# A hybrid decoder layer on one core: the first pass's places filled earlier in the queue, rotary tables and forget chain issued later, background sums spread over two stages, one place filled sooner

## The chip, the cores and the metric

The kernel runs on one core of one Trainium2 chip. The metric is the device time of one execution in microseconds. Before the change the median of three runs is 917.3 us (917.18 to 917.92).

## What is computed

A decoder layer on 512 tokens of width 2048, with two groups of eight heads side by side: FoX heads (attention with a forget term added to the logits) and MLA heads (latent attention with a rotary part). Cut to what matters:

```python
def _hybrid_layer(x, cos, sin, g_pre, w_in, g_q, w_uq, g_kv, w_ukv, b_forget, w_out, g_post):
    h = _rms_norm(x, g_pre)
    proj = h @ w_in                       # 2048 x 6472
    (q_lat, kv_lat, k_rope_raw, gate_mla,
     fq, fk, fv, f_logit, gate_fox) = jnp.split(proj, split_points, axis=-1)
    o_mla = _mla_branch(q_lat, kv_lat, k_rope_raw, g_q, w_uq, g_kv, w_ukv, cos, sin) * jax.nn.silu(gate_mla)
    o_fox = _fox_branch(fq, fk, fv, f_logit, b_forget) * jax.nn.silu(gate_fox)
    o = jnp.concatenate([o_mla, o_fox], axis=-1) @ w_out
    return x + _rms_norm(o, g_post)
# _fox_branch: log_f = log_sigmoid(f_logit + b_forget); c = cumsum(log_f);
#   logits = (q . k) * scale + c[query] - c[key], causal softmax, times v
# cos, sin: of positions * inv_freq, used in the MLA heads alone
```

## The kernel before

All of it is one straight program. TensorE runs the matmuls in fp32 split into a high and a low part, so a product is three matmuls: `mm3`, L149 (high by high), L150 and L151 (high by low, low by high). Each weight block of 128x1024 numbers ("chunk", 512 KB) goes the same way: a DMA from HBM into a tile `raw`, issued on SP's queue (`load`, L249 and L262); ScalarE (ACT) rounds it to the high part `whi` (L282, about 1.05 us); VectorE (DVE) subtracts to get the low part `wlo` (L283, about 1.2 us); then TensorE (PE) uses both. Division into parts runs two chunks ahead of the matmuls. `raw` tiles come from small pools, so a load waits until what used its place before is done. Each engine works its instructions in the order of its queue; SP, which only issues DMAs, does too. SP's DMAs share eight completion semaphores in turn, so in the built program a DMA on SP also waits for the landing of the DMA eight places before it.

Large products are done in a seven-product scheme over 2x2 blocks: products p1, p2, g5, g3, g7, q6, p4 of two operands each, where operands can be sums or differences of blocks. Sums of weight blocks are made by DMA in two ways:

- **Chains** (`add_chain`, `fill`, L232): a place in memory holds a first block, loaded by SP (L235), and later products add further blocks to the same place by an accumulating DMA on GpSimd's (POOL's) queue (L237). The first pass has eight such places per pair of outputs: v0 to v3, g0 to g3; the second pair l and m has its own.
- **Background sums** (`add_step`, L310 to L327) for blocks of w_out and w_ukv, in DRAM: 16 steps, each a small mark (SP, L327), a copy of the first block (SP, L325) and an accumulate of the second (POOL, L321). Four are narrow (named ...u), twelve move 1 MB twice (...o). `paced` lets one step go after so many weight tiles (`set_pace`; a wide one takes twice as many).

Sums of x blocks are made on DVE and stored away by POOL (L993, `awaymg`), to be fetched later (L1032).

The stages, in order of time in the trace: the opening projection (`proj_first`, tiles `in`, L645, 16 steps of k, each 12 matmuls of 128x328 and 4 transposes; the normalised x comes as `h` from ACT and then from DVE, L142), fq of head pair 0, then p1 and p2 for v and g (tiles `va`, `ga`), the other five products of v and g (`products`), fk, the FoX heads in four pairs, p1 and p2 of l and m, their other products (g5 of m is tile `mg`), the latent stage, the MLA heads in four pairs, and the output projection.

Around the change:

- `rotary_tables` (L857): SP loads the inverse frequencies (L859) and four pieces of the positions (L863); DVE then casts the positions (L870), multiplies (L871) and reduces the angle in many small steps (L877 to L905), ACT takes sines, POOL stores the tables, SP spreads them (L913). Its DMAs are written where it is called, its steps where `todo` reaches them. The scheduler that orders the program outside the sections written in fixed order may place them earlier.
- `forget_sums` (L786): the forget chain, 17 small steps on DVE and ACT with a RECIPROCAL on DVE (L829) and a store of the cumulative sums to DRAM (`c_dram`, L818), read by FoX (`load_keys`). `fs[0]` runs early, `fs[1:]` where they are put into `todo`.
- `fill` for l and m: the four places of g5's l are `slot` tiles filled after p1 of l and m (L1510); the first place of g5's m, `rawm0`, is a tile of the pool `rw`, which opens only when p2 of l is done (L1524).

Of the kernel before, what the change touches and what calls it, by code (L numbers as in the profile page):

```python
# [65 lines left out]
def tile_hybrid_layer(  # L66
# [32 lines left out]
    def slot(name, dt=F32, shape=(P, 2, S)):  # L99

        return sp.tile(list(shape), dt, tag="s", name=name)
# [127 lines left out]
    def fill(i, raw):  # L229

        raws[i] = raw
        to = raw.rearrange("p (k c) -> p k c", k=2)  # L232
        first, second = chunks[i][0]
        if first is not None:
            nc.sync.dma_start(to, first)  # L235
        if second is not None:
            pool.dma_start(to, second, accum_op=ALU.add)  # L237
# [351 lines left out]
    def set_pace(n):  # L589
        state.update(pace=n, tiles=0)  # L590
# [196 lines left out]
    def forget_sums(r):  # L787
# [5 lines left out]
        def rows():  # L793
            pool.memset(zrow, 0.0)
            pt = att_bank("rf")
            for t in range(NT):
                pe.transpose(pt[:n, t * P : (t + 1) * P], r[:, t * n : (t + 1) * n], ident)
            dve.tensor_copy(rf[:n, :], pt[:n, :])
# [16 lines left out]

        def scan():
            dve.tensor_tensor_scan(rf[R, :], z, zrow, 0.0, op0=ALU.add, op1=ALU.add)
            nc.sync.dma_start(c_dram, rf[R, :])  # L818
# [437 lines left out]
    set_pace(1000)  # L1256
    rot = rotary_tables()
    todo.append(fs[0])
# [97 lines left out]
    drain()  # L1356
    todo.extend(fs[1:])
    for g in "vg":
# [6 lines left out]
        {  # L1365
            ("g5", "v"): (1, d3), ("g5", "g"): (1, f7), ("g5", "g", "after"): lambda: todo.extend(rot),
            ("g3", "v"): (1, d7), ("g3", "g"): (1, f6), ("g7", "v"): (1, d6),
# [9 lines left out]
    pp = heads_room.enter_context(tc.tile_pool(name="pp", bufs=2, reuse_waits="tile"))  # L1377
    set_pace(3.7)
    wait(4)
# [128 lines left out]
    drain()  # L1508
    for j in range(4):
        fill(prods["g5", "l"][j], slot(f"rawl{j}", shape=(P, 1024)))  # L1510
    l4 = slot("l4b", shape=(P, NT, L4))
# [10 lines left out]
    for f in f5:  # L1522
        f()
    fill(prods["g5", "m"][0], beside[0].tile([P, 1024], F32, tag="raw", name="rawm0", bufs=1))  # L1524
    raws_of[0] = slot("lat4")
# [45 lines left out]

    set_pace(4.5)
    pp = heads_room.enter_context(tc.tile_pool(name="pp", bufs=2, reuse_waits="tile"))
# [65 lines left out]
    for p in range(4):  # L1639
# [5 lines left out]
        if p == 0:  # L1645
            set_pace(4.5)
            A = [proj_bank("uA0"), bank("pv", "uA1", 1)]
# [264 lines left out]
```

## Time and profile before

| what | value |
|---|---|
| median of three runs | 917.3 us |
| the profiled execution | 922.15 us, of which its span from first to last instruction is 920.4 us |
| PE busy | 885.9 us, 96% of the span |
| DVE, ACT, POOL busy | 634.6, 499.4, 125.4 us |
| mean granted TensorE clock | 0.981 of full speed |
| DMA queues | q1 (issued by SP): 136.28 MB; q0 (issued by POOL): 61.02 MB |

How to read it: a time in a row is microseconds from the start of the span. A row of the timeline is start, duration, engine, line, operation, output and inputs, and in brackets the idle time before it with what ended it. A row of the chain of waits is start, duration and what lies on the path that ended last; a DMA there lasts from issue to landing. A row of the stretch table gives, for a stretch of time, its length, then the busy time (and instruction count) of PE, of PE's weight loads (PEld), DVE, ACT and POOL, then the granted clock (PEclk, 1.00 is full speed), the share of time that the DMA engines were busy, and GB/s. A PE busy share of 96% does not say that PE runs at full speed for 96%: in a stretch with PEclk 0.50 it is busy with the same matmuls for twice as long.

### The profile page before, as it was taken

The numbers are of one execution on the slowest core, as the hardware profiler recorded it, in microseconds if no ns is written. First come the engines' busy times: TensorE is split into PE (matmuls) and PEld (weight loads), VectorE is DVE, ScalarE is ACT, GpSimd is POOL, SyncE is SP. The second block draws the span as 40 slices with busy tenths as digits, with TensorE's granted clock in tenths as the row PEclk, the third lists the DMA queues.
The fourth block names the chain that finished last, engine by engine and source line by source line (L and its number), as shares of the span: only waits on it lengthen the run. The fifth ranks groups of instructions, "written<-read, shape, count | busy, mean of one in ns | idle before, by whom it ended". The sixth has DMA issues, their size and how long they took to land.

```text
span 920.4 us, 13773 instructions
## 1 busy us (share of the span) xinstructions
PE 885.9 (96%) x5078; PEld 779.2 (85%) x5078; DVE 634.6 (69%) x1056; ACT 499.4 (54%) x914; POOL 125.4 (14%) x133
## 2 busy tenths in 40 slices
PE   5999989999999999899997999999999999999996
PEld 5988889999988888688997999997888888887885
DVE  2789586658455553545664766899796895888786
ACT  4764554435345362444743444566866877645473
POOL 0114102442200010100022344100000000000021
PEclk8899989999999999899999999999999999999998
DMA  8979968999799999997699999652322335788878
GB/s 266 244 214 261 254 195 197 220 227 220 179 223 292 263 257 245 254 259 219 183 301 325 308 224 206 107 164 60 104 58 73 122 100 197 233 314 304 278 223 249
DMA packets 128360, 198.41 MB, mean 216 GB/s; under 512 B 16210, under 2 KB 61164, under 8 KB 127268
## 3 DMA queue, kind: packets, MB, share of 16 engines
q1 hardware_dynamic: 101300, 136.28, 46.7%
q0 software_dynamic: 26256, 61.02, 33.5%
q8 instruction: 40, 0.66, 0.3%
q10 hardware_dynamic: 736, 0.22, 0.1%
q14 instruction: 28, 0.23, 0.1%
HBM read 182.60 MB, written 44.25 MB: 246 GB/s over the span
## 4 chain that ended last, share of the span: by engine, by line
PE 79%; DMA 10%; DVE 4%; issue 3%; ACT 2%; POOL 1%; SPq 1%; DVEq 0%; ACTq 0%; POOLq 0%
DMA raw<-in_w_in_dram 4%; DMA rawm<-in_w_in_dram 3%; PE sm L688 3%; PE fq L149 3%; PE in L645 3%; PE fq L150 3%; PE fq L151 3%; PE fk L151 2%; PE fk L149 2%; PE fk L150 2%; PE mq L149 2%; PE mq L150 2%; PE mq L151 2%; PE sf L688 2%; PE oa L151 2%
## 5 line engine op out<-in xcount | busy, mean ns | idle before, releaser
L283 DVE TENSOR_TENSOR wlo<-raw,whi 128x1024 fp32r<-128x1024 f32 (+3 forms) x159 | 186.8, 1177 | 116.7 <-ACT whi L282 116.0
L282 ACT CAST whi<-raw 128x1024 fp32r<-128x1024 f32 (+3 forms) x159 | 160.6, 1012 | 153.7 <-PE fk L150 33.7
L149 PE MATMUL fk<-h,whi 128*128 128x512 f32 x128 | 52.5, 410 | 0.0
L149 PE MATMUL fq<-h,whi 128*128 128x512 f32 x128 | 52.0, 406 | 0.0
L150 PE MATMUL fq<-h,whi 128*128 128x512 f32 x128 | 50.8, 397 | 0.0
L151 PE MATMUL fq<-h,wlo 128*128 128x512 f32 x128 | 50.7, 396 | 0.0
L151 PE MATMUL fk<-h,wlo 128*128 128x512 f32 x128 | 50.3, 393 | 0.0
L150 PE MATMUL fk<-h,whi 128*128 128x512 f32 x128 | 50.0, 391 | 0.0
L1732 POOL DMA_DIRECT2D c<-in_x_dram x8 | 7.0, 1008 | 309.0 <-ACT c L1731 309.0
L282 ACT CAST whi<-rawv 128x1024 fp32r<-128x1024 f32 x24 | 25.1, 1050 | 41.5 <-PE gc L150 9.8
L282 ACT CAST whi<-rawg 128x1024 fp32r<-128x1024 f32 x24 | 25.2, 1051 | 29.7 <-PE vc L151 8.9
L283 DVE TENSOR_TENSOR wlo<-rawv,whi 128x1024 fp32r<-128x1024 f32 x24 | 29.3, 1224 | 17.1 <-ACT whi L282 17.0
L645 PE MATMUL in<-whi,h 128*128 128x328 f32 x128 | 31.0, 329 | 8.9 <-DVE h L142 8.7
L283 DVE TENSOR_TENSOR wlo<-rawg,whi 128x1024 fp32r<-128x1024 f32 x24 | 29.3, 1223 | 14.2 <-ACT whi L282 14.2
L706 ACT ACTIVATE pf<-pf,stf 128x128 f32<-128x128 f32 (+3 forms) x32 | 18.0, 562 | 33.1 <-DVE stf L697 33.1
L282 ACT CAST whi<-rawl 128x1024 fp32r<-128x1024 f32 x20 | 21.0, 1049 | 22.2 <-PE mc L150 7.5
L283 DVE TENSOR_TENSOR wlo<-rawl,whi 128x1024 fp32r<-128x1024 f32 x20 | 24.4, 1223 | 10.2 <-ACT whi L282 10.2
L645 PEld LDWEIGHTS in<-whi,h 128*128 128x128 f32 x128 | 22.0, 193 | 9.4 <-DVE h L142 9.0
L151 PEld LDWEIGHTS fq<-h,wlo 128*128 128x128 f32 x128 | 24.6, 192 | 5.6
L149 PE MATMUL mq<-ln,whi 128*128 128x512 f32 x72 | 29.0, 403 | 0.0
L151 PEld LDWEIGHTS fk<-h,wlo 128*128 128x128 f32 x128 | 24.0, 188 | 5.3
L150 PEld LDWEIGHTS fq<-h,whi 128*128 128x128 f32 x128 | 24.7, 193 | 4.5
(635 smaller groups left out, 2963.3 us busy)
## 6 DMA issues: line engine op xcount, KB each, us to landing
raw<-in_w_in_dram SPq DMA_DIRECT2D x62, 512.0 KB, 8.9
raw<-in_w_out_dram SPq DMA_DIRECT2D x32, 512.0 KB, 4.9
rawv<-in_w_in_dram POOLq DMA_DIRECT2D x16, 512.0 KB, 6.5
rawg<-in_w_in_dram POOLq DMA_DIRECT2D x16, 512.0 KB, 9.6
rawl<-in_w_in_dram POOLq DMA_DIRECT2D x16, 512.0 KB, 9.9
raw<-in_w_in_dram POOLq DMA_DIRECT2D x12, 512.0 KB, 9.7
bmg<-awaymg SPq DMA_DIRECT2D x20, 256.0 KB, 9.4
rawv<-in_w_in_dram SPq DMA_DIRECT2D x8, 512.0 KB, 4.7
```

Of the source, the lines that this page charges most:

```text
L149: pe.matmul(o, ah, bh, start=first, stop=False, **kw)
L150: pe.matmul(o, ah, bl, start=False, stop=False, **kw)
L151: pe.matmul(o, al, bh, start=False, stop=last, **kw)
L282: act.copy(hi[:, :m], raw[:, :m])
L283: dve.tensor_tensor(out=lo[:, :m], in0=raw[:, :m], in1=hi[:, :m].bitcast(F32), op=ALU.subtract)
L645: pe.matmul(banks[t][:, :n], a[k][:, tss[t]], b[:, j, :], start=k == 0 and m == 0, stop=k == NK - 1 and m == 2,)
L688: pe.matmul(s[:, :nn], a[:, qs], c[:, :nn], start=(i == 0), stop=(i == len(pairs) - 1))
L706: act.activation(p, p, AF.Exp, bias=st[:, 0:1], scale=unit, accum_out=st[:, 1:2])
L1732: pool.dma_start(to, x[piece(t, c)], accum_op=ALU.add)
```

## The change

Six edits. The SP half of `fill` is pinned to the order in which the program is written, so the scheduler may not move it behind other DMAs. The memset of `zrow` goes from the first step of the forget chain to its last. `rotary_tables` is called, and the rest of the forget chain is queued, after product g3 of g instead of at the opening and after p1. The pace of the background sums goes from 3.7 to 6 tiles in the FoX stage and from 4.5 to 3.3 in the MLA stage (a second `set_pace(4.5)` inside the MLA loop goes away). The first place of g5's m becomes a slot and is filled together with the four of l.

```diff
@@ fill
-            nc.sync.dma_start(to, first)
+            in_order(nc.sync.dma_start(to, first))
@@ forget_sums
         def rows():
-            pool.memset(zrow, 0.0)
...
         def scan():
+            pool.memset(zrow, 0.0)
@@
     set_pace(1000)
-    rot = rotary_tables()
     todo.append(fs[0])
@@
     drain()
-    todo.extend(fs[1:])
     for g in "vg":
         one("p2", g, A[g], False, side=f3 if g == "g" else ())
@@ products("vg", {
-            ("g5", "v"): (1, d3), ("g5", "g"): (1, f7), ("g5", "g", "after"): lambda: todo.extend(rot),
+            ("g5", "v"): (1, d3), ("g5", "g"): (1, f7), ("g3", "g", "after"): lambda: todo.extend([*fs[1:], *rotary_tables()]),
@@ FoX stage
-    set_pace(3.7)
+    set_pace(6)
@@ after p1 of l and m
-    for j in range(4):
-        fill(prods["g5", "l"][j], slot(f"rawl{j}", shape=(P, 1024)))
+    for i in (*prods["g5", "l"], prods["g5", "m"][0]):
+        fill(i, slot(f"rawl{i}", shape=(P, 1024)))
@@
     for f in f5:
         f()
-    fill(prods["g5", "m"][0], beside[0].tile([P, 1024], F32, tag="raw", name="rawm0", bufs=1))
@@ MLA stage
-    set_pace(4.5)
+    set_pace(3.3)
@@
         if p == 0:
-            set_pace(4.5)
```

What this does to the order of the built program shows at three places. First SP's queue in the opening, before: `bcol` is the forget bias, `ifc` the inverse frequencies, `angles` the positions, `rawv` and `rawg` are first-pass places, `raw_152` and `raw_157` are chunks 5 and 6 of the opening projection (k = 8, 9 and k = 10, 11).

```order
L766 DMA bcol<-in_b_forget_dram 8x1
L859 DMA ifc<-in_inv_freq_dram 128x2
L863 DMA angles<-in_positions_dram 32x128 x4
L235 DMA rawv_678<-in_w_in_dram 128x2x512
L235 DMA rawv_680<-in_w_in_dram 128x2x512
L262 DMA raw_152<-in_w_in_dram 128x2x320
L262 DMA raw_152<-in_w_in_dram 128x2x8
L235 DMA rawv_682<-in_w_in_dram 128x2x512
L235 DMA rawv_684<-in_w_in_dram 128x2x512
L262 DMA raw_157<-in_w_in_dram 128x2x320
L262 DMA raw_157<-in_w_in_dram 128x2x8
L235 DMA rawg_686<-in_w_in_dram 128x2x512
```

And the same stretch of SP's queue after the change.

```order
L766 DMA bcol<-in_b_forget_dram 8x1
L235 DMA rawv_670<-in_w_in_dram 128x2x512
L235 DMA rawv_672<-in_w_in_dram 128x2x512
L235 DMA rawv_674<-in_w_in_dram 128x2x512
L235 DMA rawv_676<-in_w_in_dram 128x2x512
L262 DMA raw_152<-in_w_in_dram 128x2x320
L262 DMA raw_152<-in_w_in_dram 128x2x8
L235 DMA rawg_678<-in_w_in_dram 128x2x512
L859 DMA ifc<-in_inv_freq_dram 128x2
L262 DMA raw_157<-in_w_in_dram 128x2x320
L262 DMA raw_157<-in_w_in_dram 128x2x8
L863 DMA angles<-in_positions_dram 32x128 x4
```

The positions are still loaded in the opening, though `rotary_tables` is called much later in the text: the scheduler hoists them. They have moved from ahead of all five places to behind them and behind chunks 5 and 6.

Second, DVE's queue at the same place, before: `h3` to `h7` are the normalised x of steps k = 3 to 7, `wlo3` the low part of chunk 3 (k = 4, 5).

```order
L283 TENSOR_TENSOR wlo2_237<-raw2_135,whi2_236 128x656
L870 CAST angles_672<-angles_672 128x128
L871 TENSOR_SCALAR angles_672<-angles_672,ifc_670 128x128
L877 TENSOR_SCALAR angles_672<-angles_672 128x128
L878 TENSOR_SCALAR angles_672<-angles_672 128x128
L142 SCALAR_TENSOR_TENSOR h3_261<-xt3_256,gcol_124,h3_261 128x512
L885 SCALAR_TENSOR_TENSOR angles_672<-angles_672 128x128 x4
L877 TENSOR_SCALAR angles_672<-angles_672 128x128
L878 TENSOR_SCALAR angles_672<-angles_672 128x128
L142 SCALAR_TENSOR_TENSOR h4_285<-xt4_280,gcol_124,h4_285 128x512
L283 TENSOR_TENSOR wlo3_289<-raw3_142,whi3_288 128x656
```

And after: `h8` and `wlo5` belong to step k = 8.

```order
L283 TENSOR_TENSOR wlo3_289<-raw3_142,whi3_288 128x656
L142 SCALAR_TENSOR_TENSOR h5_313<-xt5_308,gcol_124,h5_313 128x512
L142 SCALAR_TENSOR_TENSOR h6_321<-xt6_316,gcol_124,h6_321 128x512
L283 TENSOR_TENSOR wlo4_346<-raw4_147,whi4_345 128x656
L142 SCALAR_TENSOR_TENSOR h7_354<-xt7_349,gcol_124,h7_354 128x512
L870 CAST angles_1719<-angles_1719 128x128
L871 TENSOR_SCALAR angles_1719<-angles_1719,ifc_1717 128x128
L142 SCALAR_TENSOR_TENSOR h8_378<-xt8_373,gcol_124,h8_378 128x512
L877 TENSOR_SCALAR angles_1719<-angles_1719 128x128
L878 TENSOR_SCALAR angles_1719<-angles_1719 128x128
L885 SCALAR_TENSOR_TENSOR angles_1719<-angles_1719 128x128 x3
L283 TENSOR_TENSOR wlo5_403<-raw5_152,whi5_402 128x656
```

The cast of the positions, which waits for their four DMAs, has moved on DVE's queue from ahead of `h3` to behind `h7` and ahead of `h8` and `wlo5`.

Third, POOL's queue between the FoX stage and the product `mg`, before: `t6o` and `t4o` are background sums, `rawl` the places of l, `rawm` the first place of m, `raw_4420`, `raw_4469` and `raw_4520` its second to fourth, `awayoa` and `awayog` stores.

```order
L321 DMA t6o_115<-t7o_111 128x2048
L321 DMA t4o_119<-t6o_115 128x2048
L993 DMA awayoa_4761<-gc_1106 256x1x256
L237 DMA rawl_4335<-in_w_in_dram 128x2x512
L237 DMA rawl_4338<-in_w_in_dram 128x2x512
L237 DMA rawl_4341<-in_w_in_dram 128x2x512
L237 DMA rawl_4344<-in_w_in_dram 128x2x512
L237 DMA raw_4420<-in_w_in_dram 128x2x512
L993 DMA awayoa_4907<-gc_1105 256x1x256
L993 DMA awayog_4832<-rog_4817 128x1024
L993 DMA awayog_4868<-rog_4853 128x1024
L237 DMA rawm_4578<-in_w_in_dram 128x2x512
```

And after, where `rawl_4329` is the first place of m and `raw_4405`, `raw_4454` and `raw_4505` its second to fourth.

```order
L321 DMA t7o_110<-in_w_out_dram 128x2x1024
L993 DMA awayoa_4743<-gc_1097 256x1x256
L237 DMA rawl_4317<-in_w_in_dram 128x2x512
L237 DMA rawl_4320<-in_w_in_dram 128x2x512
L237 DMA rawl_4323<-in_w_in_dram 128x2x512
L237 DMA rawl_4326<-in_w_in_dram 128x2x512
L237 DMA rawl_4329<-in_w_in_dram 128x2x512
L993 DMA awayoa_4889<-gc_1096 256x1x256
L237 DMA raw_4405<-in_w_in_dram 128x2x512
L993 DMA awayog_4814<-rog_4799 128x1024
L993 DMA awayog_4850<-rog_4835 128x1024
L237 DMA raw_4454<-in_w_in_dram 128x2x512
```

The accumulate of m's first place has moved up on POOL, past that of its second place, a store of 256 KB and two stores of 512 KB. Its third still stands behind all of those stores.

## The prediction, on record before the run

> **What bounds the kernel now.** First the page.
>
> ```profile
> span 920.4 us, 13773 instructions
> PE 885.9 (96%) x5078; PEld 779.2 (85%) x5078; DVE 634.6 (69%) x1056; ACT 499.4 (54%) x914; POOL 125.4 (14%) x133
> ```
>
> TensorE (PE) is the bound, so an edit can pay only where PE waits or runs at a lower clock. The view of waits, for PE alone, says where: engine, line and awaited work, then microseconds in total, times, longest.
>
> ```profile
> PE in L645 <- DVE h L142: 8.7, 1, 8.7
> PE mg L149 <- ACT whi L282: 5.3, 1, 5.3
> PE ga L151 <- DVE wlo L283: 2.4, 1, 2.4
> PE pvf L149 <- ACT phf L138: 2.3, 1, 2.3
> ```
>
> Four single stalls stand out, 18.7 us together. The table of stretches shows that they cost more than that.
>
> ```profile
> 17.86:28.10 10.24, 4.04 (x17) 4.00 (x17) 5.35 (x16) 0.59 (x1) 0.00 (x0) 0.50 0.87 275
> 116.84:123.67 6.83, 5.68 (x26) 5.68 (x27) 5.84 (x7) 1.93 (x3) 0.88 (x2) 0.50 0.61 194
> ...
> 111.40:128.84 17.44, 14.62 (x96) 14.04 (x95) 15.04 (x17) 7.49 (x10) 1.44 (x2) 0.80 0.62 204
> 315.58:320.52 4.94, 4.94 (x27) 4.16 (x25) 4.94 (x11) 2.49 (x5) 0.00 (x0) 1.00 1.05 248
> 369.05:381.09 12.04, 8.80 (x27) 6.65 (x26) 7.69 (x19) 4.46 (x10) 1.57 (x2) 0.72 0.97 281
> 487.20:498.62 11.42, 11.42 (x98) 11.42 (x96) 5.02 (x6) 3.93 (x6) 3.63 (x3) 1.00 1.07 342
> 498.62:518.40 19.78, 14.04 (x99) 13.55 (x98) 12.87 (x16) 8.26 (x10) 2.46 (x4) 0.83 1.08 326
> ...
> 667.00:745.00 78.00, 77.37 (x392) 64.37 (x391) 65.24 (x135) 57.62 (x141) 0.00 (x0) 1.00 0.27 82
> 262.00:369.00 107.00, 107.00 (x511) 88.80 (x510) 56.27 (x126) 51.49 (x109) 9.19 (x10) 1.00 0.99 259
> ```
>
> The first two rows are half-clock stretches (PEclk 0.50): each stall is followed by one, and a stretch of 6.83 us at half clock loses 3.4 us of work. The next five are products with and without their stall. A product of 96 matmuls of this size takes 11.42 us at full speed (`lg`, 487.20). `ga` of p2 (111.40) took 17.44, so its stall and low clock cost 6.0. The FoX piece at 369.05 took 12.04 against 4.94 for the same 27 matmuls a pair earlier: 7.1. `mg` (498.62) took 19.78: 8.4.
>
> The trace and a rule differ here: the stall of 2.4 us in `ga` was enough to bring 6.83 us at clock 0.50. The Trainium skill, page "TensorE: Matmul & The Clock Gate", section "HAM oscillation — how this bites in real kernels", gives as abstract rule that idle gaps over some 3.4 us are to be avoided; this row shows a shorter one doing it. By that rule a leftover stall below 3.4 us would cost only its own length; by the row it can cost 3.4 more.
>
> **Opening: the stall moves.** Rows of the chain of waits, of the timelines of PE, DVE and SP, and of the DMA view from 15.5 to 19 us.
>
> ```profile
> 18.51 3.68 DMA angles<-in_positions_dram
> 34.98 1.77 PE in L645 x12
> 37.19 1.80 PE in L645 x12
> ...
> 14.47 0.85 PE L645 MATMUL in<-whi,h 128*128 128x328 f32 x4
> 24.06 1.46 PE L645 MATMUL in<-whi,h 128*128 128x328 f32 x4 [8.74 <-DVE h L142]
> ...
> 22.27 0.23 DVE L870 CAST angles<-angles 128x128 f32<-128x128 int32 x1 [9.80 <-DMA angles<-in_positions_dram]
> 23.26 0.74 DVE L142 SCALAR_TENSOR_TENSOR h<-xt,gcol,h 128x512 fp32r<-128x512 f32 x1
> 23.92 1.26 DVE L885 SCALAR_TENSOR_TENSOR angles<-angles 128x128 f32<-128x128 f32 x4
> 26.28 0.83 DVE L283 TENSOR_TENSOR wlo<-raw,whi 128x656 fp32r<-128x656 f32 x1
> ...
> 20.00 1.80 SPq L235 DMA_DIRECT2D rawv<-in_w_in_dram  x2
> ...
> DMA packets 1267, 1.21 MB, mean 346 GB/s; under 512 B 81, under 2 KB 1267, under 8 KB 1267
> ```
>
> DVE stood 9.80 us at the cast of the positions, whose DMAs lay behind x on SP's queue until 22.19 (18.51 + 3.68); the x of step k = 3 stood behind the cast, and PE behind that, from 15.3 to 24.06. After the change the cast stands behind `h7`, so k = 3 to 7 run without it. A step takes 2.21 us (34.98 to 37.19), so k = 8 could start at 15.3 + 5 x 2.21 = 26.4 instead of 37.19: 10.8 us, if nothing else held it. But the positions now stand on SP's queue behind five places of 512 KB and two chunks of 336 KB, 3.29 MB; at 346 GB/s that is 9.5 us. Added to the old landing, 31.7; if the whole 3.68 us of their own issue and landing overlapped with it, 28.0. I take 30. The Trainium skill, page "DMA: Bandwidth & Descriptors", section "Anatomy of one DMA", fits 2.0 us plus bytes at 436 GB/s for a DMA from the other queue; as an estimate that is 7.5 us for the 3.29 MB, and the term below would be about 4 instead of 2; this row, with 346 GB/s in small packets, is slower.
>
> From the cast DVE needs 1.73 us to the end of an `h` (22.27 to 24.00, with L871 to L878 between), 0.95 for three L885 (1.26 x 3/4) and 0.83 for `wlo5`: 3.5. So `wlo5`, which k = 8 needs for its second matmul, is there at 33.5. The half clock then goes on, as before (28.10 is 4.0 us after 24.06, which lost 2.0). So k = 8 stands where it would have started at about 35.5, against 37.19: **a gain of 1.7**, from -1 (31.7 and a longer half clock) to 5 (28.0 and a shorter one). ACT's sines and the table store come later in the opening, beside running matmuls; nothing for those.
>
> **p2 of g.** Rows of the chain, of the timelines of SP, POOL and DVE, and of the DMA view at 93.2 us.
>
> ```profile
> 98.23 11.66 DMA awaymg<-rmg
> 110.42 4.78 DMA raw<-in_w_in_dram
> ...
> 97.39 14.72 SPq L249 DMA_DIRECT2D raw<-in_w_in_dram  x5
> ...
> 93.26 0.59 POOL L993 DMA_DIRECT2D awaymg<-rmg  x1
> ...
> 113.33 3.35 DVE L829 RECIPROCAL fd<-fd 8x512 f32<-8x512 f32 x1
> ...
> awaymg<-rmg POOLq DMA_DIRECT2D x1, 512.0 KB, 11.1
> ```
>
> Of the five loads from 97.39 on, the last three left SP only after the last away store had landed (98.23 + 11.66 = 109.89), because the third one's place overlaps that store's. One of them, issued at 110.42, landed at 115.2, and DVE was then in the forget chain's RECIPROCAL until 116.68. In the changed program the places fall otherwise: the chunk for the start of `ga` waits for the store before (93.26 + 11.1 = 104.4), the next two only for DVE, and the fourth alone for 109.89. With the 4.78 us of the row it lands by 114.7, and the fourth quarter of `ga` starts at 111.40 + 3 x 2.85 = 119.95, with 1.05 us of rounding ahead. The chain of RECIPROCAL is gone from here. **Gain 5.5**, bounds 0 (the same queue delay meets the second quarter) and 6.0.
>
> The forget chain now runs in product g7. One row on the room there.
>
> ```profile
> 175.00:205.00 30.00, 30.00 (x179) 26.82 (x178) 19.07 (x21) 12.46 (x14) 13.66 (x12) 1.00 1.11 223
> ```
>
> DVE is idle for 10.9 of 30 us and division runs two chunks (5.7 us) ahead, so 3.35 us hide: 0, at worst 1. FoX reads the sums only after two more products, q6 and p4.
>
> **FoX.** One row of the chain:
>
> ```profile
> 345.44 24.86 DMA raw<-in_w_in_dram
> ```
>
> This load took 24.86 us from issue to landing while the DMA engines were busy 0.99 of the time (262 to 369). It shares them with a background step. At pace 6 instead of 3.7 there are 38% fewer of these; seven of the twelve wide steps stay in FoX. PE waited 2.3 us and a little more behind it, so 21 us would be soon enough: 16% less. **Gain 6.5** of 7.1; bounds 0 (what holds it is SP's own queue, with keys and values ahead) and 7.1.
>
> **m's first place.** Rows of the chain, of POOL's timeline and of the DMA view at 461.3 and 465.8 us.
>
> ```profile
> 476.54 10.89 DMA rawm<-in_w_in_dram
> 488.03 14.94 DMA rawm<-in_w_in_dram
> ...
> 461.40 1.21 POOL L237 DMA_DIRECT2D rawl<-in_w_in_dram  x1 [29.04 <-PE ptf L715]
> 463.21 3.87 POOL L237 DMA_DIRECT2D rawl<-in_w_in_dram  x3 [0.59 <-DMA rawl<-in_w_in_dram]
> ...
> rawl<-in_w_in_dram POOLq DMA_DIRECT2D x1, 512.0 KB, 9.9
> ...
> rawl<-in_w_in_dram POOLq DMA_DIRECT2D x1, 512.0 KB, 17.4
> ```
>
> The first of four accumulates for l landed at 471.3, the fourth at about 483.3: 4.0 us each. A fifth in that row lands at 487, 11 us before `mg` starts, instead of 502.97. What is late next: the third place of m, which stood one behind `rawm`, comes about where that came, 503.0, and the fourth 4.0 later, 507. Needed, with rounding ahead, at 498.62 + 2 x 2.85 - 1.05 = 503.3 and 506.1, `wlo` a little tighter: some 2 us of small stalls. **Gain 6**, bounds 3 (a half-clock stretch follows them) and 8.4.
>
> **Background sums in the MLA stage.** Five wide steps, 10 MB, move into 612 to 745. There DMA is busy 0.27 of the time with 82 GB/s and PE runs at clock 1.00; 10 MB over 133 us add 79 GB/s, so bandwidth suffices. A load behind a 1 MB copy on SP's queue is 1.05 MB / 346 GB/s = 3 us later, and a mark makes SP wait for a rounded chunk, with the loads of the next chunks queued behind. **Cost 2**, from 0 to 15 (3 us shown five times); nearer zero, since that much DMA time is idle. Loads in FoX are relieved by the same steps, counted above. `zrow` and the lost second `set_pace` change nothing by themselves.
>
> **The sum.** 1.7 + 5.5 + 6.5 + 6 - 2 = 17.7 us. The profiled execution, 922.15 us (span 920.4 and 1.75 around it), would become 904.5. The median of the runs, 917.3, lies 4.85 below it; I take off the same: 899.6, say 900. What a measurement can tell from no change is about 0.2%, 1.8 us.
>
> **Rivals.**
> - *The opening's stall goes altogether.* The positions land before DVE has done `h7`, at 26 or so. For it: they are four small DMAs, and SP issued the first pair of places only at 20.00, when x was nearly done. Against: the built order has them last of 3.29 MB. Then 10.8 instead of 1.7: 917.3 - 26.8 = 890.5. Chance 0.12.
> - *Stalls move rather than go.* FoX's load stays late behind SP's own keys and values (0 for 6.5), and the fourth place of m brings a half-clock stretch (3 for 6): 8.2, so 909. For it: DMA is at 0.99 there with or without a third of the sums. Chance 0.18.
> - *Slower: the MLA stage becomes bound by loads.* Each of the five copies delays a load by 3 us; where two chunks ahead don't cover that, PE stalls for 2.4 or more and pays 3.4 at half clock, about 6 each. It decides from four of the five on, since the other terms hold 19.7. All five: 30 - 19.7 = 10 slower, 927. Against: PE there is 77.37 of 78.00 busy at clock 1.00. Chance 0.06.
> - *It doesn't do what it says.* The rotary tables "later" are still loaded in the opening, as the order shows; if the rest too only changes places, with as many stalls as before, the time is within 0.2%, 917. Chance 0.04.
>
> The forecast itself has 0.60, with 895 to 905 as its own range from the bounds of its terms taken together. The range 889 to 911 takes in the first two rivals and leaves out 0.1 for the others and some of the edges. Faster by over 0.2%: 0.60 + 0.12 + 0.18, less 0.02 for the edges, 0.88; within: 0.05; slower: 0.07.
>
> **What would show it.** In the profile after: PE's wait in `in` (L645) is one of 6 to 8 us, near 26 to 34 us instead of 15 to 24, with the cast L870 starting near 30. `ga` L151 leaves the list of waits and the `ga` stretch is near 11.5 to 12. No half-clock stretch lies near 370, and the FoX load takes under 21 us. `mg` takes 12 to 15 us. Clock in the MLA stage stays 1.00 with a DMA share near 0.5. Wrong it would be made by a cast that starts before 26, by a load in FoX that still takes over 22 us, or by new waits of over 2 us on `mq`, `mk` or `uA`.

## The result

The changed kernel took 914.64 us in the median of 20 runs (911.76 to 916.32), the kernel before, timed beside it, 919.17 us (median of 20): ratio 0.994, 95% interval 0.9925 to 0.9955. That is 5.5 us faster by the ratio and 4.5 by the two medians. One execution of the kernel before took 2229.54 us, far outside all others, and does not show in either. Beside the last experiments the same two kernels were timed again on one chip: ratio 0.9951 (0.9932 to 0.997). The forecast was 900 us with a range from 889 to 911: the direction was right, the size three to four times too large, and the time lies above the range.

The two profiled executions differ by more, 922.15 against 913.19 us, or 9.0. The one of before lies 3.0 above its median of 20 and the one after 1.45 below its own. The accounts below are of this pair, so their sum is 9, not 4.5 or 5.5.

### The profile page after: what moved, and what is told of

Its sections match the earlier page's. It is cut to its first block, busy times and chain, and to the rows that moved or that the text cites. A ratio compares the mean times of both kernels' runs of the same rounds, so it can differ in the third digit from the quotient of the medians.

```text
span 911.3 us, 13774 instructions
## 1 busy us (share of the span) xinstructions
PE 881.8 (97%) x5078; PEld 775.2 (85%) x5078; DVE 634.9 (70%) x1056; ACT 500.7 (55%) x915; POOL 125.4 (14%) x133
## 4 chain that ended last, share of the span: by engine, by line
PE 85%; DMA 5%; DVE 5%; ACT 3%; issue 1%; SPq 1%; DVEq 0%; ACTq 0%
PE fq L149 3%; PE fk L151 3%; PE fk L149 3%; PE fk L150 3%; PE fq L151 3%; PE fq L150 3%; PE sm L688 3%; DMA raw<-in_w_in_dram 3%; PE mq L149 2%; PE mq L150 2%; PE mq L151 2%; PE oc L149 2%; PE oa L151 2%; PE oa L150 2%; PE oc L151 2%; PE oc L150 2%
## 5 line engine op out<-in xcount | busy, mean ns | idle before, releaser
L282 ACT CAST whi<-rawl 128x1024 fp32r<-128x1024 f32 x25 | 26.2, 1048 | 31.1 <-PE mc L150 7.5
L283 DVE TENSOR_TENSOR wlo<-rawl,whi 128x1024 fp32r<-128x1024 f32 x25 | 30.5, 1223 | 18.0 <-ACT whi L282 18.0
L237 POOL DMA_DIRECT2D rawl<-in_w_in_dram x20 | 23.8, 1192 | 53.5 <-PE ptf L715 31.2
L151 PE MATMUL mq<-ln,wlo 128*128 128x512 f32 x72 | 28.4, 394 | 0.0
```

The source lines that it names most:

```text
L151: pe.matmul(o, al, bh, start=False, stop=last, **kw)
L282: act.copy(hi[:, :m], raw[:, :m])
L283: dve.tensor_tensor(out=lo[:, :m], in0=raw[:, :m], in1=hi[:, :m].bitcast(F32), op=ALU.subtract)
```

## The profile after

The page of the changed kernel begins:

```profile
span 911.3 us, 13774 instructions
```

TensorE's waits in the changed kernel, longest first:

```profile
PE in L645 <- DVE wlo L283: 5.1, 2, 4.8
PE in L645 <- ACT whi L282: 3.4, 1, 3.4
PE gc L149 <- DVE gc L1296: 2.4, 2, 1.2
...
PE lg L149 <- ACT whi L282: 1.5, 1, 1.5
PE vc L150 <- DVE wlo L283: 1.5, 1, 1.5
```

Three of the four big waits of before are gone: `mg`, `pvf`, and most of `ga`. The opening's is still there, in two parts. New are `gc`, `vc` and `lg`.

To see where the time went, the program is cut at starts of products, and each piece measured in both. The stretch table of before (length first, then busy times, and the granted clock as the third figure from the end) for p2 of v and g, for g7 and q6, for the FoX heads, for p1 of l to the end of `mg`, and for the MLA heads to the output:

```profile
99.92:128.96 29.04, 25.96 (x146) 23.09 (x145) 19.65 (x22) 14.24 (x17) 1.44 (x2) 0.88 0.68 215
173.80:218.64 44.84, 44.84 (x290) 41.05 (x289) 30.50 (x36) 19.75 (x24) 20.87 (x19) 1.00 1.11 226
...
289.76:430.33 140.57, 137.33 (x646) 113.35 (x645) 69.64 (x150) 63.58 (x134) 12.32 (x14) 0.98 0.97 258
430.33:518.52 88.19, 82.43 (x652) 80.86 (x651) 57.19 (x95) 47.73 (x82) 14.84 (x16) 0.96 0.90 271
612.01:911.56 299.55, 296.23 (x1398) 244.39 (x1397) 246.17 (x428) 196.37 (x388) 7.70 (x9) 1.00 0.55 173
```

The same five pieces after the change:

```profile
98.29:123.09 24.80, 23.24 (x147) 20.51 (x145) 11.55 (x10) 10.33 (x13) 1.91 (x3) 1.00 0.92 284
167.93:219.24 51.31, 47.47 (x290) 42.33 (x289) 41.63 (x49) 23.84 (x28) 21.23 (x20) 0.97 0.99 194
...
290.36:424.22 133.86, 133.86 (x647) 111.17 (x645) 69.79 (x150) 63.65 (x134) 8.73 (x10) 1.00 0.80 211
424.22:509.75 85.53, 81.95 (x652) 80.34 (x650) 56.37 (x94) 47.71 (x82) 14.57 (x15) 0.98 0.89 267
603.24:902.35 299.11, 296.03 (x1398) 244.58 (x1397) 246.01 (x428) 196.23 (x388) 11.96 (x14) 1.00 0.72 208
```

| piece | before | after | measured gain | forecast |
|---|---|---|---|---|
| opening and fq, up to p1 | 77.53 | 75.90 | 1.6 | 1.7 |
| p2 of v and g | 29.04 | 24.80 | 4.2 | 5.5 |
| g7 and q6 (forget chain's new place) | 44.84 | 51.31 | -6.5 | 0 |
| FoX heads | 140.57 | 133.86 | 6.7 | 6.5 |
| p1 of l to the end of `mg` | 88.19 | 85.53 | 2.7 | 6 |
| MLA heads to the output | 299.55 | 299.11 | 0.4 | -2 |
| sum | | | 9.1 | 17.7 |

The sum of the pieces is the difference of the spans, 920.4 - 911.3. The rows to look at are the second of each table: the same 290 matmuls, VectorE busy 41.63 instead of 30.50 us. VectorE's own timeline of the changed kernel shows how:

```profile
190.68 1.23 DVE L283 TENSOR_TENSOR wlo<-rawv,whi 128x1024 fp32r<-128x1024 f32 x1
191.94 3.34 DVE L829 RECIPROCAL fd<-fd 8x512 f32<-8x512 f32 x1
195.32 0.69 DVE L139 TENSOR_TENSOR bmq<-bmq 128x512 fp32r<-128x512 f32 x1
196.04 0.68 DVE L805 TENSOR_TENSOR fw<-fw,fd 8x512 f32<-8x512 f32 x1
196.75 0.69 DVE L1296 TENSOR_TENSOR gc<-gc,gc 128x512 f32<-128x512 f32 x1
197.47 0.68 DVE L805 TENSOR_TENSOR fw<-fw,fz 8x512 f32<-8x512 f32 x1
198.08 0.41 DVE L800 TENSOR_SCALAR fd<-fw 8x512 f32<-8x512 f32 x1
198.52 0.69 DVE L1296 TENSOR_TENSOR gc<-gc,gc 128x512 f32<-128x512 f32 x1
199.24 0.68 DVE L805 TENSOR_TENSOR fd<-fd,fz 8x512 f32<-8x512 f32 x1
199.96 1.23 DVE L283 TENSOR_TENSOR wlo<-rawv,whi 128x1024 fp32r<-128x1024 f32 x1
```

There is no bracket in these rows: VectorE does not pause between 190.68 and 201. Steps whose tile begins with `f` at 8x512 are the chain's. Between two low parts of chunks (190.68 and 199.96) lie 8 us of other work, 5.8 of it the chain's. The two stores `gc` at 196.75 and 198.52 take product g7 out of the banks that q6 needs, and they stand behind the chain, hence TensorE's wait `gc <- gc`; then it waits for the low part of 199.96 (`vc <- wlo`).

## The experiments

Each is one or two edits against a kernel named there; the labels e1 to e11 are those that the expectations use. A tick is a point between matmuls at which the program takes the next queued step. The ratio is always to the kernel before on the same chip, and its interval is 0.003 to 0.006 wide, as large as many single effects here; so a stage is read from its piece of the profiled execution, where one piece repeats closely (the piece of g7 and q6 took 51.31, 51.77 and 52.58 us in three kernels that are alike there).

**The forget chain back in p2** (e1, against the changed kernel).

```diff
+    todo.extend(fs[1:])      # after p1, as before
-    ("g3", "g", "after"): lambda: todo.extend([*fs[1:], *rotary_tables()])
+    ("g3", "g", "after"): lambda: todo.extend(rotary_tables())
```

> The changed kernel with one edit: the rest of the forget chain is queued after p1 again, as before the change; the rotary tables stay queued after g3. Theory: the chain's small steps and its 3.34 us RECIPROCAL on VectorE are what holds back the stores of product g7 and the chunk parts of q6 (28.9 us from the start of q6's v to the start of p4's v, where before needed 22.4). Then this stretch falls back to 22.4 to 23, TensorE's waits for DVE gc go, the half-clock stretch near 202 goes, and the time is about 6 us shorter than the changed kernel: ratio to before near 0.987 to 0.989. The chain then runs beside p2 of g, where the loads now come earlier, so that stretch stays below 14 us. Rival: the loads and accumulates of those chunks are late and VectorE only waits with them. Then the stretch stays above 25 us and the ratio near 0.994.

Measured: ratio 0.9941 (0.9917 to 0.9966), no change that can be told from the changed kernel. The pieces p2 and g7 with q6 of this kernel:

```profile
98.08:128.69 30.61, 24.97 (x146) 22.04 (x145) 22.54 (x25) 14.37 (x17) 2.57 (x4) 0.94 0.68 210
173.53:218.37 44.84, 44.84 (x290) 41.05 (x289) 29.71 (x35) 20.12 (x24) 20.68 (x19) 1.00 1.12 231
```

g7 and q6 are back at 44.84, so the theory holds there: the chain's place costs 6.5. But the ratio is the one that the rival named, for another reason: p2 went from 24.80 to 30.61, and `ga` alone took 17.5, though I had it below 14. VectorE's timeline in that stretch:

```profile
108.82 0.42 DVE L800 TENSOR_SCALAR fw<-fz 8x512 f32<-8x512 f32 x1 [3.98 <-DMA awaymg<-rmg]
...
114.06 3.34 DVE L829 RECIPROCAL fd<-fd 8x512 f32<-8x512 f32 x1
117.43 2.36 DVE L283 TENSOR_TENSOR wlo<-raw,whi 128x1024 fp32r<-128x1024 f32 x2
```

The chain waits for the last away store (the bracket at 108.82; in the built program its tile `fw` lies where that store's source lay), so its RECIPROCAL comes at 114 and two low parts come right behind it. The loads of this kernel stand earlier on SP's queue, as in the changed one, and p2 is no shorter than before (29.04). So the earlier loads that I had named first win nothing as long as the chain stands there; it is the chain's leaving that shortens p2. Whether that would have been enough with the late loads of before, no run shows.

**m's first place late again** (e2, against the changed kernel).

```diff
-    for i in (*prods["g5", "l"], prods["g5", "m"][0]):
-        fill(i, slot(f"rawl{i}", shape=(P, 1024)))
+    for j in range(4):
+        fill(prods["g5", "l"][j], slot(f"rawl{j}", shape=(P, 1024)))
...
+    fill(prods["g5", "m"][0], beside[0].tile([P, 1024], F32, tag="raw", name="rawm0", bufs=1))
```

> The changed kernel with one edit: m's first place is filled late, from the small pool, as before the change. Theory: the early fill both saves the wait before mg (5.8 us between lg and mg) and costs about 3 us ahead of lg, since 512 KB more stand before the loads of p2 of l and the fetches on SP's queue. Then lg starts without a stall, mg loses 6 to 8 us, and the net is 2 to 3 us slower than the changed kernel: ratio to before near 0.997. Rival: what is late ahead of lg has nothing to do with the early fill. Then those stalls of about 3 us stay and the whole wait before mg comes on top: 6 us or more slower, ratio 1.000 or over.

Measured: 0.9998 (0.9983 to 1.0013). `ma` is the tile of p2 of m, `lg` that of g5 of l. From the last `ma` stretch to `lg`, `lg`, and the wait with `mg`:

```profile
470.36:481.95 11.59, 11.59 (x99) 11.59 (x97) 7.85 (x11) 7.50 (x12) 3.04 (x4) 1.00 1.08 324
481.95:493.35 11.40, 11.40 (x97) 11.40 (x96) 4.93 (x6) 3.83 (x6) 3.65 (x3) 1.00 1.07 340
493.35:512.67 19.32, 13.62 (x100) 13.13 (x99) 12.88 (x16) 8.16 (x10) 2.57 (x4) 0.82 1.08 323
```

The same three in the changed kernel:

```profile
471.00:484.27 13.27, 11.76 (x100) 11.56 (x98) 6.70 (x10) 6.15 (x10) 3.08 (x4) 1.00 1.09 302
484.27:498.23 13.96, 13.20 (x97) 13.00 (x97) 9.46 (x10) 7.50 (x10) 2.45 (x2) 0.88 1.08 324
498.23:509.75 11.52, 11.52 (x99) 11.52 (x97) 9.59 (x13) 6.18 (x8) 2.36 (x3) 1.00 1.07 355
```

In the profile the theory holds: with the late fill the first two are clean and the third loses 7.8; with the early one the third is clean and the first two lose 1.7 and 2.6. Another 1.3 is lost before them, in two waits of the last FoX heads (`pvf`, 0.3 and 1.0 us, at 464.68 and 469.88). The whole piece from p1 of l takes 87.80 against 85.53 here, so by the profile the early fill is worth 2.3. The ratio says more, 0.006 or 5 us, which comes near what the rival had; the profiled spans differ by 2.7 (914.0 and 911.3). I go by the piece, and what makes up the rest of the ratio stays open.

**Paces back** (e3, against the changed kernel).

```diff
-    set_pace(6)
+    set_pace(3.7)
...
-    set_pace(3.3)
+    set_pace(4.5)
...
+            set_pace(4.5)
```

> The changed kernel with one edit: the pace of the background sums as before (3.7 in FoX, 4.5 in the MLA stage, with the second setting). Theory: the FoX load that took 24.86 us was late because of the background sums, so the stall near 370 with its half-clock stretch comes back: 5 to 7 us slower than the changed kernel, ratio near 1.000. Rival: it was late by the place of the sums in time, or by the order of SP's queue, which the other edits have shifted anyway; then no load takes over 21 us, no half-clock stretch lies between 300 and 400, and the time stays within 2 us of the changed kernel. In both cases the MLA stage stays as it is (its clock 1.00).

Measured: 1.0016 (0.9992 to 1.0039). The FoX piece, and the load of which the chain of waits now speaks:

```profile
291.66:432.78 141.12, 137.00 (x646) 113.04 (x645) 69.63 (x150) 63.59 (x134) 12.32 (x14) 0.98 0.95 258
...
352.32 20.84 DMA raw<-in_w_in_dram
```

141.12 against 133.86, and 140.57 before: the stall comes back with the background sums and with nothing else. The load took 20.84 us, under my limit of 21, and TensorE stalled all the same. The limit measured the wrong thing: this load was issued at 352.32, 60.7 us after the start of the piece, the one before the change at 345.44, 55.7 after it. What counts is when a load lands, and that is its issue and its time together: 81.5 and 80.5 us after the start. The DMA engines are 0.95 busy here and 0.80 in the changed kernel.

**The cast of the positions pinned** (e4, against e1, the kernel with the chain back in p2).

```diff
         def angles():
-            dve.tensor_copy(n1, r.bitcast(I32))
+            in_order(dve.tensor_copy(n1, r.bitcast(I32)))
```

> The kernel e1 with one edit more: the cast of the positions is pinned to where the program text puts it, so it and the steps that need it run on VectorE after product g3, and the tables are made there; the loads stay. Theory: two things hold step k = 8 of the opening, the cast (31.17) and chunk 5, which stands behind four places and is rounded at 28.33. With the cast gone the wait ends near 30 instead of 34.6, and the opening gains 4 to 5 us over e1, ratio lower by 0.005. Rival: the 26 small steps of the tables cost on VectorE in product g7 what they no longer cost in the opening, as the forget chain did: then TensorE waits 2 us or more for VectorE between 165 and 215 and the ratio stays within 0.002 of e1.

Measured: 0.9881 (0.9858 to 0.9905), the first clear gain over the changed kernel. TensorE in the opening of the changed kernel, with the cast on VectorE, and then TensorE in this one:

```profile
29.12 0.64 PE L645 MATMUL in<-whi,h 128*128 128x328 f32 x1 [3.36 <-ACT whi L282]
34.56 0.64 PE L645 MATMUL in<-wlo,h 128*128 128x328 f32 x1 [4.81 <-DVE wlo L283]
...
31.17 0.23 DVE L870 CAST angles<-angles 128x128 f32<-128x128 int32 x1 [10.12 <-DMA angles<-in_positions_dram]
```

```profile
29.04 0.64 PE L645 MATMUL in<-whi,h 128*128 128x328 f32 x1 [3.15 <-ACT whi L282]
29.91 0.64 PE L645 MATMUL in<-wlo,h 128*128 128x328 f32 x1 [0.24 <-DVE wlo L283]
```

The wait at k = 8 is two waits one behind the other: for chunk 5, which stands behind the places (ScalarE began to round it at 28.33 in the changed kernel, after 5.13 us of waiting for its load), and for the cast. With the cast gone the second goes, and p1 starts at 71.70 instead of 75.90 (75.69 in e1). The 25 steps of the tables on VectorE, now in g7, cost nothing: that piece stays at 44.84 us. VectorE has 35.35 us of work in it then, against 41.63 with the chain.

**No RECIPROCAL** (e5, against the changed kernel; the reciprocal is left out, and a multiplication by one stands for it).

```diff
-            lambda: dve.reciprocal(d, d),
+            number(d, d, 1.0, ALU.mult),
```

> The changed kernel with one instruction replaced: the RECIPROCAL of the forget chain (8x512, 3.34 us on VectorE) is a multiplication by one (some 0.42 us); it leaves out the reciprocal, so the forget term is not the reference's. Theory: this one long instruction, in VectorE's queue ahead of the stores of product g7, makes TensorE wait. Then the time from the start of g7's v to the start of p4's v, 51.3 us in the changed kernel and 44.8 before, falls to 46 or less, without a half-clock stretch near 200. Rival: it is the sum of the chain's fifteen steps of 0.4 to 0.7 us in a stage where VectorE is busy: then it stays above 48 us.

Measured: 0.9945 (0.9925 to 0.9966).

```profile
168.74:216.42 47.68, 45.41 (x290) 41.03 (x289) 38.61 (x49) 23.85 (x28) 21.23 (x20) 1.00 1.05 203
```

47.68 lies between the two expectations: of the 6.5 us, 3.6 hang on the RECIPROCAL and 2.8 on the rest of the chain.

**The chain thin over g5 and g3** (e6, against e4, the kernel with the cast pinned).

```diff
-    todo.extend(fs[1:])
...
+    for f in fs[1:]:         # after p2, every second tick
+        todo.append(f)
+        wait(1)
```

> The kernel e4 with one edit: the forget chain is queued after p2, one step for every second tick, so over g5 and g3 of both v and g, where VectorE is busy for 28 of 45 us. Theory: the chain costs TensorE nothing where it is thin enough and no away store stands before it; p2 of g takes about 12.7 us as in the changed kernel, and the four products of g5 and g3 take 44.8 us: 3 to 4 us less than e4, ratio lower by 0.004. Rival: the RECIPROCAL alone holds back a chunk's low part wherever it stands: then the four products take 47 us or more, and the ratio stays within 0.002 of e4.

Measured: 0.993 (0.9908 to 0.9953), no better: by the ratios worse, by the spans (906.5 against 905.4) by 1 us. p2, then g5 and g3, the wait that is new, and VectorE where it ends:

```profile
93.20:115.62 22.42, 22.42 (x147) 20.53 (x146) 11.42 (x12) 13.53 (x17) 1.46 (x2) 1.00 0.82 255
115.62:169.51 53.89, 46.32 (x291) 42.23 (x289) 39.32 (x43) 21.93 (x26) 11.50 (x11) 0.94 0.83 189
...
PE gg L149 <- DVE gc L1298: 7.6, 1, 7.6
...
154.59 1.22 DVE L817 TENSOR_TENSOR_SCAN rf<-fz,fd 8x512 f32<-8x512 f32 x1
155.84 1.29 DVE L1298 TENSOR_TENSOR gc<-gg,gc 128x512 f32<-128x512 f32 x2
```

p2 without the chain, and begun 5 us earlier, runs at full speed (22.42). But g5 and g3 lose 9, with one wait of 7.6 us and a half-clock stretch: the store of g5 (`gc`) stood on VectorE behind the scan that ends the chain. My rival named a chunk's low part; it is a store, as in g7, but held for another reason. In e4 the same store ran at 145.14, as the product ended; here the product ended near 138 and its store came at 155.84. In the built program of this kernel the tiles of `gc` lie where the chain's tiles `fz` and `fd` lie, so the store has to wait until the scan has read them; in the kernels before, after, e1, e4 and e11 they lie elsewhere. So this run says what a shared memory place costs, and not what a thin chain costs.

**m's first place filled after p2 of l's loads** (e7, against e6, the thin-chain kernel).

```diff
-    for i in (*prods["g5", "l"], prods["g5", "m"][0]):
+    for i in prods["g5", "l"]:
         fill(i, slot(f"rawl{i}", shape=(P, 1024)))
...
     one("p2", "l", A["l"], False, 2)
+    fill(prods["g5", "m"][0], slot("rawm0", shape=(P, 1024)))
```

> The kernel e6 with one edit: m's first place is still a slot, but is filled after the loads of p2 of l have been queued. Theory: what costs 3 us ahead of lg in the changed kernel is that the fifth fill stands on both queues before the loads and accumulates that p2 and lg need. Then lg starts without a stall (11.6 us from the last ma to lg instead of 13.3), and the place lands just before mg, between 487 and 497: gain 2 to 4 us over e6. Rival: the place then lands too late again, since its accumulate stands behind that of the second place: mg waits 3 us or more and the sum is no better than e6.

Measured: 0.9937 (0.9914 to 0.9959), the same. The piece from p1 of l to the end of `mg` takes 86.08 against 85.66 us. `lg` (first row) has lost its stall, and `mg` (second row) shows it instead:

```profile
477.34:489.37 12.03, 11.66 (x97) 11.46 (x96) 6.02 (x7) 5.06 (x8) 3.28 (x4) 1.00 1.08 310
489.37:506.10 16.73, 13.07 (x100) 11.95 (x98) 11.20 (x14) 7.83 (x10) 1.29 (x3) 1.00 1.07 336
```

So the rival holds. In this stretch the DMA engines are at 1.07 to 1.09 in every row shown (the view adds up the time of single packets, so the share can pass 1): in the orders tried here, a place filled sooner made another later.

**Chunk 5 in a place of its own** (e8, against e6, the thin-chain kernel).

```diff
-        if i < 2:
+        if i < 2 or i == 5:
             raw = slot(f"raw{i}", shape=(P, 1024))
```

> The kernel e6 with one edit: chunk 5 of the opening projection (k = 8, 9) gets a place of its own, so its load needs no earlier chunk to be done and stands ahead of the four first-pass places on SP's queue. Theory: with the cast out of the opening, what is left at k = 8 is chunk 5 behind 2 MB of places (rounded at 28.3). Then the wait of 3.4 us with its half-clock stretch goes, and p1 starts 6 to 7 us earlier than in e6: ratio lower by 0.006. Rival: the next chunk, 6, now stands behind the places and is as late: the same wait at k = 10, and the gain is under 2 us.

Measured: 0.994 (0.9917 to 0.9962), nothing gained. The wait at k = 8 is gone, and another has come where fq begins, with a half-clock stretch of its own:

```profile
45.42 0.77 PE L149 MATMUL fq<-h,whi 128*128 128x512 f32 x1 [2.57 <-ACT whi L282]
...
45.48:48.89 3.41, 3.35 (x7) 2.24 (x8) 2.87 (x12) 2.68 (x5) 0.00 (x0) 0.50 0.49 129
```

p1 starts at 70.90, against 70.80 without the edit. Neither theory had that: the wait moved past the opening altogether. What holds the first chunk of fq I did not try.

**RECIPROCAL in four, in the changed kernel (e9); in four, in p2 (e10); and in four, thin, with the tables ahead (e11).** The second is against e4, the kernel with the cast pinned, the third against the second.

```diff
-            lambda: dve.reciprocal(d, d),
+            *(lambda c=c: dve.reciprocal(d[:, c : c + P], d[:, c : c + P]) for c in range(0, S, P)),
@@ third kernel alone
-    todo.extend(fs[1:])                       # after p1
+    todo.extend(rotary_tables())              # after p2
...
-    ("g3", "g", "after"): lambda: todo.extend(rotary_tables())
+    ("g3", "g", "after"): lambda: todo.extend(s for f in fs[1:] for s in (f, lambda: None))
```

> The changed kernel with one edit: the forget chain's RECIPROCAL of 8x512 is four of 8x128 in steps of their own. Theory: about half of the 6.5 us that the chain costs in g7 and q6 comes from one instruction of 3.34 us that nothing can pass on VectorE; four pieces of 0.85 us let chunk parts and stores in between. Then the time from g7's v to p4's v falls from 51.3 to 46 to 49 us. Rival: VectorE is simply full there with the chain, in whatever pieces: then it stays above 50.5 us.

Measured: 0.995 (0.9934 to 0.9966). The piece of g7 and q6 takes 51.84 us, against 52.58 in the changed kernel beside it:

```profile
167.99:219.83 51.84, 48.43 (x291) 42.93 (x289) 41.90 (x52) 23.83 (x28) 21.22 (x20) 0.93 1.01 204
```

The rival holds: in this place, at one step a tick, pieces don't help. Three of the four still ran in a row, 2.57 us together.

> The kernel e4 (chain after p1, cast pinned) with the same edit: four RECIPROCALs of 8x128. Theory: the 3.0 us wait of ga for a chunk's low part, with its half-clock stretch, comes from the long instruction; in pieces it goes, and the time from p2's v to g5's v falls from 29.1 to 25 or 26 us, where the changed kernel, without the chain there, has 24.8. The time is 3 to 4 us below e4: ratio lower by 0.004. Rival: the pieces follow each other on VectorE just ahead of the same chunk, because the built order puts three of them in a row; the wait stays above 2 us.

Measured: 0.9845 (0.9817 to 0.9873). p2 of v and g:

```profile
94.22:120.50 26.28, 23.54 (x147) 20.63 (x145) 18.66 (x22) 14.05 (x17) 1.98 (x3) 1.00 0.66 207
```

26.28 against 29.14 with the long instruction, and the half-clock stretch in it is gone (clock 1.00 for 0.94). Here the theory holds.

> The kernel e10 with chain and tables changed over: the tables' steps run after p2 (in g5 and g3), the forget chain after g3 on every second tick only (over g7 and q6, RECIPROCAL in four). Theory: thin and in pieces the chain costs nothing there; p2 takes 24.8 us and g5 to q6 89.7 us, so this is the shortest of all, 3 us or more below e10. Rival: steps of the chain or of the tables hold memory places or stores that the products need, as in e6; then a wait of over 2 us shows up in g5 to q6 and nothing is won over e10.

Measured: 902.97 us, ratio 0.9829 (0.9802 to 0.9855), the fastest here and faster than both kernels by more than the intervals; from e10 the intervals do not part it. p2, then g5 to q6:

```profile
93.94:116.50 22.56, 22.56 (x147) 20.61 (x146) 10.83 (x9) 10.26 (x13) 1.46 (x2) 1.00 0.94 302
116.50:208.03 91.53, 90.32 (x579) 81.99 (x577) 72.83 (x103) 46.66 (x55) 32.82 (x30) 1.00 1.00 218
```

g5 to q6 take 91.53 us, where two pairs of clean products are 2 x 44.84 = 89.7 and the changed kernel has 44.84 + 51.31 = 96.2. The same chain, thin and in pieces, costs under 2 us there: g5 and g3 with the tables take 44.84, g7 and q6 with the chain 46.69, and no wait in them is over 1.2 us, so the rival fails (one more wait of 0.8 us lies in p4, `vp`). e9 has the pieces without the thinning and wins nothing; thinning with the RECIPROCAL whole was not run in this place. The profiled gain over the kernel with the chain in p2 is 1.8 us (spans 901.4 and 903.2); I had expected 3.

> The changed kernel as it is, beside e9 to e11 on the same chip, for the size of the difference between chips: ratio to before of 0.992 to 0.996 expected by every theory.

Measured: 0.9951 (0.9932 to 0.997), as expected.

## Why the prediction was wrong

- **Opening: right in its mechanism, to a tenth by luck.** Cast at 31.17 (I took 30), TensorE's second matmul of k = 8 at 34.56 (33.5), 1.6 us gained for 1.7, though both came over 1 us later than I had them; in another execution of the same kernel p1 starts at 76.77, a gain of 0.8. The stall moved, as the built order says. What I did not see is that chunk 5 itself was late as well; the pinned cast shows it. The rival of an opening without a stall failed for the reason given.
- **The forget chain: the step that failed.** The prediction had "DVE is idle for 10.9 of 30 us and division runs two chunks (5.7 us) ahead, so 3.35 us hide: 0, at worst 1". It cost 6.5, the largest miss in the sum; e1, with the chain elsewhere, has the piece back at 44.84. Three things were wrong in it. I priced the RECIPROCAL and not the chain: VectorE's work in the piece grew by 11.1 us (41.63 - 30.50), 3.34 of them the RECIPROCAL's. I compared it with an average idle share over 30 us, though a thing queued in order hides only in the gaps where it stands. And I looked only at chunk parts, while the stores of finished products stand in the same queue and TensorE waits for the banks that they free, with no lead of two chunks.
- **p2 of g: size nearly right (4.2 for 5.5), reason wrong.** I put the stall down to three late loads first and the chain second. With the loads where the change puts them and the chain back in its old place, p2 takes 30.61, no less than before (29.04). The gain came with the chain's leaving, and so the two terms are one: the chain's 6 us were moved from p2 to g7, with nothing won by the move (ratio 0.994 with and without it).
- **FoX: right.** 6.7 for 6.5, and the pace alone brings the stall back. The limit of 21 us that stood behind it was not the right measure, as e3 shows.
- **m's first place: the wait went wholly (`mg` in 11.52 us, where I had left 2 of stalls), and over 5 of its 8 us were lost again ahead of it.** This term had the right mechanism and about double the size. The prediction asked what is late next in the queue behind the place, and not what stood there before and was now behind it: the loads of p2 of l and the fetches for `lg`. e7 bears that out, since `lg` loses its stall when the place is filled behind those loads. Measured 2.7 for 6.
- **Background sums in the MLA stage: no cost, for 2.** The DMA share there rose from 0.55 to 0.72 over the whole piece, and TensorE's time did not.
- **From the profile to the median.** I took the same 4.85 us off the profiled execution as before. The profiled execution lay 3.0 above its median before, and 1.45 below it after. This alone takes 4.4 of the 9.0 us, and one profiled execution against the median of three runs was not enough to know it.

Added up, the time came out 15.0 us above the 899.6 of the sum. The terms of the stages make 8.7 of that (chain 6.5, m's place 3.3, p2 1.3, less 2.4 for the MLA stage, the rest roundings), the step from the profile to the median 6.3 (4.85 + 1.45). Without the chain's 6.5 us, or without the 6.3 of that last step, the time would lie inside the range; the chain is the step of the mechanism that failed.

None of the rivals had the chain. "Stalls move rather than go" is nearest in kind, but it put them into FoX, which came out as forecast. And most signs that the prediction named did come: the cast at 31, no half clock near 370, `mg` in 11.5 us, no wait of over 2 us on `mq`, `mk` or `uA`. No sign looked at g7 and q6, where the time was lost.

On the clock: in g7 and q6 three waits of TensorE of 1.2 to 1.5 us, close together, were followed by this stretch.

```profile
201.86:205.27 3.41, 3.41 (x10) 2.67 (x9) 3.29 (x5) 0.00 (x0) 2.01 (x2) 0.50 0.57 75
```

The prediction's doubt about the rule of 3.4 us idle (the Trainium skill, page "TensorE: Matmul & The Clock Gate", section "HAM oscillation — how this bites in real kernels") is borne out once more: none of the three waits was half as long. The stretch of one window, 3.41 us, agrees with what that page's section "What's actually happening" gives as the window's length. But a short wait does not always bring a half-clock stretch: without the RECIPROCAL (e5) TensorE waited 2.10 us once in the same piece and the granted clock stayed at 1.00, and its waits of 1.5 and 0.8 us for `lg`, followed by a half-clock stretch in the changed kernel, were followed by none there. What decides between the two, these runs do not show.

## What to carry to other kernels

Moving a chain of small work off one stage is worth something only if the stage that takes it has gaps where the chain will stand; price the whole chain, in the queue, with everything behind it, stores of finished banks included. Thin it out and cut its long instruction: the same chain cost about 6 us in two places and under 2 when it was both thin and in pieces, while pieces alone won nothing in g7 and 2.9 us in p2. Look, too, at whose memory places the moved chain now holds (e6 lost 9 us to that). Where the DMA engines are full, filling one place sooner can make another late, so ask both what is late behind the moved transfer and what it has overtaken.

## What was not expected of the hardware

A RECIPROCAL of 8x512 takes VectorE 3.34 us, five times a TENSOR_TENSOR of the same shape (0.68), and four of 8x128 took 0.89 to 0.95 each, 3.5 together (e9). With only 8 of 128 partitions in use, 8x512 costs as much as the 128x512 of the same kind beside it (0.69). Nineteen of the 20 runs of the unchanged kernel before lay between 917.2 and 925.3 us, so differences of single profiles under some 5 us say little about the time, while a stage's own piece repeats within about 1.3 us.
